# Output product of a gated convolution: sums of weights on VectorE, the last pair's operands kept in SBUF, first halves of x loaded, weights split up to eleven products ahead

## The chip, the cores and the metric

The kernel runs on one core of a Trainium2 chip, as one launch. The metric is the device time in microseconds. The engines have names as in the profile: PE is TensorE (PEld its weight loads), DVE is VectorE, ACT is ScalarE, POOL is GpSimd, SP is the engine whose queue issues most loads.

## The reference, cut to what matters

A decoder trunk of two layers in float32, with 1024 positions and width 1024. Layer 0 has a short gated convolution as its mixer, layer 1 a dilated attention; each is followed by a SwiGLU FFN of width 2816. The change is in layer 0's mixer alone:

```python
def short_conv_mixer(h, w_in, conv_k, w_out):
    b, c, u = jnp.split(h @ w_in, 3, axis=-1)
    y = lax.conv_general_dilated(c * u, ...)      # depthwise, causal, three taps
    return (b * y) @ w_out
# in the trunk:  x = x + short_conv_mixer(rms_norm(x, mix_norm[0]), ...)
#                x = x + swiglu(rms_norm(x, ffn_norm[0]), ...)
```

What is changed is `(b * y) @ w_out`, a product of 1024 x 1024 by 1024 x 1024, and the addition of its result to `x`.

## The kernel before, in words

**Precision.** Every float32 operand is split into a high and a low part of a narrower type (`hi`, `lo`). A product takes three matmuls: high by high, high by low, low by high (lines 656, 657, 658). `split` makes the parts of a weight: ScalarE copies the high part (line 159), VectorE subtracts it to get the low part (line 160). `hi` does the same for operands (lines 648 and 649).

**Fast products.** The large products use a Strassen-Winograd scheme: a 2 x 2 block product is done with seven products, m = 1 to 7, instead of eight. Each of the seven needs sums of blocks of the weights and sums of blocks of the operand. Rows of x and of the operand go in two halves of 512 columns ("half 0" and "half 1").

**The convolution's output product** (`down` in class `Strassen`, with key `conv`). The operand `b * y` has 8 tiles, taken as four pairs q = 0 to 3. For each pair the sums of operands for m = 4 to 7 are made by VectorE in `store` (lines 828 and 830), and all seven tiles of the pair are written to DRAM by POOL's queue (`put`, line 843, tensor `part_conv`). `feed` loads them back through SP's queue, one tile ahead (`hin`, line 865), and splits them into the operand of TensorE (`b`). The loop runs over the seven products in the order `DOWN = (1, 2, 6, 7, 4, 5, 3)`, and in each over four columns k = 0, 2, 4, 6. That makes 28 groups. One group is 12 matmuls of 128x128 by 128x512. In a group the program order is: make the weights that are due (`take`, `ensure`, four weights ahead), the matmuls, the addition of the bank to x (`add`, line 894 on ScalarE where it is the first to write that half of x, line 896 on VectorE otherwise), the rest of the convolution's own work (`drain`), one step of `feed` for the next m, and `after`.

**Weights of this product.** `add_summed` lets DMA make the sums of weight blocks. Two pages per column pair are loaded through SP's queue (line 239), and POOL's queue then adds other blocks onto them with accumulating DMAs (line 235), each after the last use of what was there before. The FFN's down product makes its sums with VectorE (`add_pair`, `combo`, line 267) from blocks loaded as they are (`raw`, line 191), each sum one weight ahead of its use.

**x.** The convolution's product consumes x before it is added to, so x comes from DRAM again: half of the first halves as plain loads through SP's queue, the rest as accumulating DMAs of POOL's queue onto the product's result (line 886).

**Into the FFN.** `after` is `entry`: after the products m = 2, 4, 5, 3 it squares the finished half tile of x (line 532), stores x to DRAM (`spill`), adds up squares, and in the last groups makes the FFN's first operands (`hcol`, line 1336, then `b`). There it also calls for FFN weights.

**Memory and order.** Each engine works through its own instructions in the order written. There are 41 pages of 128 x 1024 floats and, in this stage, 20 half pages; a new tile takes a free one and waits until its former readers are done. Queues of loads keep their order too: a load that waits for a page or for data holds up those behind it.

Of the kernel before, what the change touches and what calls it, by code (L numbers as in the profile page):

```python
# [13 lines left out]
ALU = mybir.AluOpType  # L14
# [7 lines left out]
KT = D // 128  # L22
# [28 lines left out]
FFN_PAIRS, FFN_CHUNK = 9, 3  # L51
DOWN = (1, 2, 6, 7, 4, 5, 3)
CONV_PAIRS, CONV_CHUNK = 4, 4
LEAD = 4
CONV_FEED = {(11, 7): 2, (11, 4): 1, (11, 3): 1}
CONV, QK = "conv", "qk"
QK_PAIRS = 8
# [58 lines left out]
def trunk(ctx: ExitStack, tc: tile.TileContext, x, gains_in, cwi, ck, cwo, wqkv, wo, relb,  # L116
          wg, wu, wd, oneh, ident, out):
    nc = tc.nc
# [56 lines left out]
    raw_src, raw_tile, raw_state = [], {}, [0]  # L175
    ops, made, op_state = [], {}, [0, 0]
    combos, raw_base, sums_of = {}, {}, {}
    fetch_of, fetched = {}, [0]

    def width(src):  # L180
        return math.prod(src.shape[1:])
# [15 lines left out]

    def ensure(upto):
        while op_state[0] < min(upto + 1, len(ops)):
            while fetched[0] < min(op_state[0] + 1 + LEAD, len(ops)):  # L200
                if ops[fetched[0]][0] in fetch_of:
                    fetch_of.pop(ops[fetched[0]][0])()
                fetched[0] += 1
            key = ops[op_state[0] + 1][0] if op_state[0] + 1 < len(ops) else None
            if key in sums_of:
                sums_of.pop(key)()
            made[op_state[0]] = ops[op_state[0]][1]()
            op_state[0] += 1
# [11 lines left out]
    def add_slab(key, src):  # L220
        i = len(raw_src)
        raw_src.append(src)
        ops.append((key, lambda: split(get_raw(i)[:, :width(src)])))

    def add_summed(u, ab, cd, w):


        t = {}
        block = lambda src, h: view(src, h * w, [[1, w]])
        twice = lambda src: view(src, 0, [[0, 2], [1, w]])  # L230
        pair = lambda p: view(p, 0, [[w, 2], [1, w]])
        rows = (cd.offset - ab.offset, 2)

        def accumulate(dst, src):
            nc.gpsimd.dma_start(out=dst, in_=src, accum_op=ALU.add)

        def load(name):
            t[name] = page("summed")
            nc.sync.dma_start(pair(t[name]), twice(ab) if name == "a" else view(ab, w, [rows, [1, w]]))

        def part(m):
            p = t["a" if m in (1, 7, 6, 3) else "b"]
            left, right = p[:, :w], p[:, w:2 * w]
            out = split(left if m in (1, 2, 7) else right, None, nc.vector)
            if m == 1:
                accumulate(pair(p), twice(cd))
            elif m == 2:
                accumulate(t["a"][:, w:2 * w], block(cd, 1))
            elif m == 6:
                accumulate(right, block(ab, 1))  # L250
            elif m == 4:
                accumulate(right, block(cd, 0))
            if m in (5, 3):
                del t["a" if m == 3 else "b"]
            return out

        fetch_of["m", u, 1], fetch_of["m", u, 2] = lambda: load("a"), lambda: load("b")
        return {m: (("m", u, m), lambda m=m: part(m)) for m in WINOGRAD}

    def add_pair(u, rows, w, eng, upto, low=(), sub=ALU.subtract):  # L260

# [139 lines left out]
    def add_down(i, w):  # L401

        at = 0
        for c, qs in enumerate(chunks[CONV] if i == CONV else laid):
            n, r = len(chunks[i][c]), len(raw_src)
            span = n * 128
            src = lambda t: (w[t][:, at * 128:(at + 2 * n) * 128] if n == len(qs) else
                             view(w[t], at * 128, [[len(qs) * 128, 2], [1, span]]))
            if i == CONV:
                units = [add_summed((i, c, 2 * u), src(2 * u), src(2 * u + 1), span) for u in range(4)]  # L410
            else:
                raw_src.extend(src(2 * u + v) for v in range(2) for u in range(4))
                upto = lambda m, r=r, u=0: r + {1: 4 + u, 2: 7, 5: 8 + u, 3: 11}.get(m, 7)
                units = [add_pair((i, c, 2 * u), (r + u, r + 4 + u), span, nc.vector,
                                  lambda m, r=r, u=u: upto(m, r, u), sub=ALU.add) for u in range(4)]
            ops.extend(t[m] for m in DOWN for t in units)
            at += 2 * len(qs)
        if not plain[i]:
            return
        place = paired(FFN_PAIRS, FFN_CHUNK, FT)  # L420
        first, step = place.index(plain[i][0]), place.index(plain[i][1]) - place.index(plain[i][0])
        assert [place[first + step * j] for j in range(4)] == list(plain[i])
        for n in range(KT):
            add_slab(("d", i, n), view(w[n], first * 128, [[step * 128, 4], [1, 128]]))
# [197 lines left out]
    class Strassen:  # L622
# [4 lines left out]
        def __init__(self, key, norm, nu, chunks, plain, source):  # L627
            self.key, self.norm, self.nu = key, norm, nu
            self.early = key in (CONV, QK)
            self.order = unit_order(nu, self.early)  # L630
            self.chunks, self.source = chunks, source
            self.b = {m: [None] * 4 for m in range(1, 8)}
            self.parts = {(q, m): dram.tile([128, HALF], F32, name=f"part_{key}_{q}_{m}")
                          for q in chain(*chunks) for m in range(1, 8)}
            self.plain = {f: dram.tile([128, S], F32, name=f"plain_{key}_{f}") for f in plain}
            self.st, self.quads, self.hid, self.deep = {}, {}, {}, {}
            self.banks, self.there, self.after = set(), set(), None
            self.lead = 1 if key == CONV else 2
            self.ahead, self.now = 2, 0

# [170 lines left out]
        def store(self, q, c, g):  # L811
# [10 lines left out]
            b11, b12, b21, b22 = (self.quads.pop((q, d)) for d in ((0, 0), (0, 1), (1, 0), (1, 1)))  # L822
            t = {}

            def make(m, a, b, less=False):
                t[m] = half_page("sum")
                if less:
                    nc.vector.scalar_tensor_tensor(t[m], a, -1.0, b, op0=ALU.mult, op1=ALU.subtract)
                else:
                    nc.vector.tensor_tensor(out=t[m], in0=a, in1=b, op=ALU.subtract)  # L830
                self.put(q, m, t[m])
# [8 lines left out]
            make(4, t[6], b21, True)  # L840

        def put(self, q, m, t):
            nc.gpsimd.dma_start(self.parts[q, m], t)
            self.there.add((q, m))

        def load_x(self, *ns):
            for n in ns:
# [3 lines left out]
        def feed(self, ahead=4):  # L851

            tiles = [(c, m, k) for c, qs in enumerate(self.chunks) for m in DOWN for k in range(len(qs))]
            raw, pair, n = {}, [], 0
            for i, (c, m, k) in enumerate(tiles):
                while n < min(i + 1 + ahead, len(tiles)):
                    d, mm, j = tiles[n]
                    if d or self.key == CONV:
                        raw[n] = half_page("hin")
                    else:  # L860
                        if j % 2 == 0:
                            pair = page("hin")
                        raw[n] = pair[:, half(j % 2)]
                    assert (self.chunks[d][j], mm) in self.there
                    nc.sync.dma_start(raw[n], self.parts[self.chunks[d][j], mm])
                    n += 1
                if k == 0:
                    self.b[m] = [None] * len(self.chunks[c])
                self.hi(m, k, raw.pop(i))()
                yield  # L870
            yield from self.feed_last()

# [7 lines left out]
        def down(self, c, feed):  # L880
# [6 lines left out]

            def add(n, h, b):
                fresh = c == 0 and (n, h) not in done
                if c == 0 and X[n] is None:  # L890
                    X[n] = page("x")
                done.add((n, h))
                if fresh and not (one and (n % 2, h) == (1, 0)):
                    nc.scalar.activation(X[n][:, half(h)], b, AF.Copy, scale=-1.0 if n % 2 else 1.0)
                else:
                    nc.vector.tensor_tensor(out=X[n][:, half(h)], in0=X[n][:, half(h)], in1=b,  # L896
                                            op=ALU.subtract if n % 2 else ALU.add)

            for i, m in enumerate(DOWN):
                d = c + (i + self.lead) // len(DOWN)  # L900
                steps = range(len(self.chunks[d])) if d < len(self.chunks) else (0, 2)
                for k in range(0, KT, 2):
# [2 lines left out]
                    if m == 5:  # L905
                        r[k] = bank()
                    b = bank() if m == 2 else r[k] if m in (3, 5) else p[k]
                    self.mm((c, k), m, b, m in (1, 2, 5), 4)
                    n, h = k + (m in (5, 7, 4)), int(m in (6, 5, 7, 3))
                    add(n, h, b)  # L910
                    if c == 0 and m in ((1, 6, 7) if one else (2, 4, 5, 3)):
                        source(n, h, nc.gpsimd, accum_op=ALU.add)
                    if one and m == 1:
                        X[n + 1] = page("x")
                        source(n + 1, 0, nc.sync)
                    if m == 4:
                        del p[k]
                    self.drain(c, m, k)
                    if k // 2 in steps:
                        next(feed, None)  # L920
                    if self.after:
                        self.after(c + 1 - len(self.chunks), m, k)

# [12 lines left out]
        def run(self, start, hooks={}):  # L936
# [25 lines left out]
                self.idle(n)  # L962

            prep = []
            feed = self.feed(1 if self.key == CONV else 4)
            self.products(filled, hooks)
            for c in range(len(self.chunks)):
                self.down(c, feed)
# [1198 lines left out]
```

## Time and profile before

| what | value |
|---|---|
| median of 3 runs | 2109.78 us (2109.09 to 2111.74) |
| the profiled execution's own time | 2111.59 us |
| its span in the profile | 2109.2 us |
| PE busy | 2070.2 us (98%), 10906 matmuls |
| DVE busy | 1774.8 us (84%) |
| ACT busy | 1049.3 us (50%) |
| POOL busy | 302.3 us (14%) |
| DMA moved | 317.23 MB, mean 150 GB/s |

The output product of the convolution lies between about 243 and 344 us of the span. A row of a timeline gives start, duration, engine, line, operation, output and inputs, and in brackets how long the engine stood idle before it and what ended that. A row of windows gives a stretch, its length, the busy time of each engine with its instructions, the granted clock of TensorE (1.00 is full), the share of the DMA engines and GB/s. [...]

### The profile page before, as it was taken

Reading aid. Unit: us, or ns where it says so; the run is one execution under the profiler, and the core shown is the slowest. Engines: PE = TensorE matmul, PEld = TensorE weight load, DVE = VectorE, ACT = ScalarE, POOL = GpSimd, SP = SyncE. Lnnn points to the kernel's source line nnn. Section 1 sums busy time; section 2 is a strip of 40 time slices with the busy share of each in tenths; the row PEclk is TensorE's granted clock in tenths of the full one; section 3 lists DMA queues with packets and bytes.
Section 4 is the critical chain, followed back from the end, with each engine's and each line's share of the span. In section 5 each row is a group of like instructions: output and inputs, shape, how many; then the busy total and the mean of one; then the engine's idle time right before and its main releaser. Section 6 shows DMA issues by size and latency. Waiting matters only on the chain.

```text
span 2109.2 us, 30920 instructions
## 1 busy us (share of the span) xinstructions
PE 2070.2 (98%) x10906; PEld 1780.5 (84%) x10906; DVE 1774.8 (84%) x3334; ACT 1049.3 (50%) x1946; POOL 302.3 (14%) x421
## 2 busy tenths in 40 slices
PE   9999887999999999999999999999999999999998
PEld 7888675888888888888889999998888888888887
DVE  8898758998888897888985888987998888887896
ACT  7433346534344355536544666665644434355443
POOL 1000320001010011010222333221011101012000
PEclk9999998999999999999999999999999999999999
DMA  7333893223333288634566868956223333368532
GB/s 220 95 100 101 242 289 92 85 81 112 103 107 107 99 261 238 200 92 149 169 238 186 196 167 217 238 182 182 69 85 110 102 109 106 110 210 230 160 100 80
DMA packets 141609, 317.23 MB, mean 150 GB/s; under 512 B 16348, under 2 KB 47150, under 8 KB 141456
## 3 DMA queue, kind: packets, MB, share of 16 engines
q1 hardware_dynamic: 98304, 203.51, 32.4%
q0 software_dynamic: 35520, 97.06, 16.0%
q10 hardware_dynamic: 7632, 14.70, 1.9%
q8 instruction: 86, 1.41, 0.3%
q14 instruction: 67, 0.55, 0.1%
HBM read 218.38 MB, written 87.65 MB: 145 GB/s over the span
## 4 chain that ended last, share of the span: by engine, by line
PE 91%; DMA 3%; DVE 3%; ACT 1%; issue 1%; POOL 0%; SPq 0%; DVEq 0%; ACTq 0%; POOLq 0%
PE bank L658 21%; PE bank L656 21%; PE bank L657 21%; PE bank L1761 5%; PE bank L748 3%; PE bank L751 3%; PE bank L750 3%; PE bank L458 2%; PE bank L460 2%; PE bank L459 2%; PE bank L1630 1%; PE bank L1632 1%; PE bank L1631 1%; PE bank L1687 1%; PE bank L1686 1%
## 5 line engine op out<-in xcount | busy, mean ns | idle before, releaser
L656 PE MATMUL bank<-b,w 128*128 128x512 f32 x2176 | 852.2, 392 | 20.9 <-ACT b L648 18.9
L657 PE MATMUL bank<-b,w 128*128 128x512 f32 x2176 | 851.5, 391 | 6.8 <-DVE b L649 6.5
L658 PE MATMUL bank<-b,w 128*128 128x512 f32 x2176 | 849.8, 391 | 2.0 <-DVE w L160 1.9
L656 PEld LDWEIGHTS bank<-b,w 128*128 128x128 f32 x2176 | 410.5, 189 | 108.2 <-ACT b L648 21.5
L657 PEld LDWEIGHTS bank<-b,w 128*128 128x128 f32 x2176 | 410.3, 189 | 95.0 <-DVE b L649 10.1
L658 PEld LDWEIGHTS bank<-b,w 128*128 128x128 f32 x2176 | 410.3, 189 | 89.5 <-DVE w L160 4.4
L159 ACT ACTIVATE w<-combo 128x512 fp32r<-128x512 f32 (+2 forms) x496 | 259.0, 549 | 271.7 <-DVE combo L267 230.0
L662 ACT ACTIVATE part<-bank 128x512 f32<-128x512 f32 x192 | 114.5, 596 | 399.2 <-PE bank L658 397.4
L160 DVE TENSOR_TENSOR w<-combo,w 128x512 fp32r<-128x512 f32 (+2 forms) x496 | 286.4, 590 | 30.9 <-ACT w L159 30.7
L160 DVE TENSOR_TENSOR w<-raw,w 128x512 fp32r<-128x512 f32 (+2 forms) x324 | 180.2, 577 | 37.9 <-ACT w L159 37.8
L666 DVE TENSOR_TENSOR part<-part,bank 128x256 f32<-128x256 f32 (+1 forms) x372 | 175.0, 499 | 32.0 <-PE bank L658 18.3
L159 ACT ACTIVATE w<-raw 128x512 fp32r<-128x512 f32 (+2 forms) x324 | 162.0, 532 | 15.3 <-PE bank L751 10.2
L649 DVE TENSOR_TENSOR b<-hin,b 128x512 fp32r<-128x512 f32 x168 | 114.4, 685 | 40.1 <-ACT b L648 40.0
L896 DVE TENSOR_TENSOR x<-x,bank 128x512 f32<-128x512 f32 x152 | 103.8, 683 | 32.0 <-PE bank L658 30.8
L267 DVE TENSOR_TENSOR combo<-raw 128x512 f32<-128x512 f32 (+1 forms) x176 | 116.1, 660 | 0.0
L648 ACT ACTIVATE b<-hin 128x512 fp32r<-128x512 f32 x168 | 103.3, 619 | 24.0 <-DMA hin<-part_conv 15.6
L751 PE MATMUL bank<-b,w 128*128 128x256 f32 x288 | 81.5, 283 | 0.0
L750 PE MATMUL bank<-b,w 128*128 128x256 f32 x288 | 81.5, 283 | 0.0
L748 PE MATMUL bank<-b,w 128*128 128x256 f32 x288 | 81.3, 282 | 0.0
L458 PE MATMUL bank<-w_hi,w 128*128 128x512 f32 (+1 forms) x208 | 76.4, 368 | 0.0
L459 PE MATMUL bank<-w_lo,w 128*128 128x512 f32 (+1 forms) x208 | 74.4, 357 | 0.0
L460 PE MATMUL bank<-w_hi,w 128*128 128x512 f32 (+1 forms) x208 | 74.4, 357 | 0.0
(239 smaller groups left out, 3270.9 us busy)
## 6 DMA issues: line engine op xcount, KB each, us to landing
hin<-part SPq DMA_DIRECT2D x140, 256.0 KB, 4.4
raw<-in_ffn_w_gate SPq DMA_DIRECT2D x44, 512.0 KB, 3.8
raw<-in_ffn_w_up SPq DMA_DIRECT2D x44, 512.0 KB, 3.8
part<-sum POOLq DMA_DIRECT2D x80, 256.0 KB, 2.3
raw<-in_attn_w_qkv SPq DMA_DIRECT2D x27, 512.0 KB, 5.4
raw<-in_conv_w_in SPq DMA_DIRECT2D x24, 512.0 KB, 4.3
raw<-in_ffn_w_down SPq DMA_DIRECT2D x32, 384.0 KB, 4.8
part<-part POOLq DMA_DIRECT2D x40, 256.0 KB, 2.5
```

Source lines behind the costliest of these rows:

```text
L159: nc.scalar.activation(hi, src, AF.Copy)
L160: low = lambda: eng.tensor_tensor(out=lo, in0=src, in1=hi, op=ALU.subtract)
L458: nc.tensor.matmul(b, whi[:, a], ahi[:, s], start=first, stop=False)
L459: nc.tensor.matmul(b, whi[:, a], alo[:, s], start=False, stop=False)
L460: nc.tensor.matmul(b, wlo[:, a], ahi[:, s], start=False, stop=last)
L656: nc.tensor.matmul(b, hi[:, a], bhi, start=start and k == 0, stop=False, skip_group_check=True)
L657: nc.tensor.matmul(b, hi[:, a], blo, start=False, stop=False, skip_group_check=True)
L658: nc.tensor.matmul(b, lo[:, a], bhi, start=False, stop=k == n - 1, skip_group_check=True)
L666: nc.vector.tensor_tensor(out=t, in0=t, in1=b, op=ALU.add)
L748: nc.tensor.matmul(b, hi[:, a], bhi, start=i in (1, 2, 5) and k == 0, stop=False, skip_group_check=True)
L750: nc.tensor.matmul(b, hi[:, a], blo, start=False, stop=False, skip_group_check=True)
L751: nc.tensor.matmul(b, lo[:, a], bhi, start=False, stop=k == n - 1, skip_group_check=True)
```

## The change

- `add_summed` and its loads go. The weights of the output product are loaded as they are (eight blocks of 512 KB), and VectorE makes the sums with `add_pair`, as it does for the FFN's down product.
- The last pair (`near`) isn't written to DRAM and read back: its operand tiles stay in SBUF, the four sums of m = 4 to 7 in two pages of their own, and `feed` takes them from there. `feed` loads four tiles ahead instead of one.
- All eight first halves of x are loaded through SP's queue at the start of `down`, and VectorE adds the products m = 1, 2 and 4 to them. The second halves stay as they were (ScalarE writes, POOL's queue accumulates).
- In this product weights are made 4, 5, 7, 9, 11, 11, 11 ahead, by product in the order of `DOWN`, at most up to operation 31 counted from the product's first, that is four weights into the FFN.
- In the groups of m = 6 `feed` makes two steps instead of one.

```diff
-LEAD = 4
+AHEAD, AHEAD_TO = (4, 5, 7, 9, 11, 11, 11), 31
...
-            while fetched[0] < min(op_state[0] + 1 + LEAD, len(ops)):
-                if ops[fetched[0]][0] in fetch_of:
-                    fetch_of.pop(ops[fetched[0]][0])()
-                fetched[0] += 1
...
-    def add_summed(u, ab, cd, w):
...
-            if i == CONV:
-                units = [add_summed((i, c, 2 * u), src(2 * u), src(2 * u + 1), span) for u in range(4)]
-            else:
-                raw_src.extend(src(2 * u + v) for v in range(2) for u in range(4))
-                upto = lambda m, r=r, u=0: r + {1: 4 + u, 2: 7, 5: 8 + u, 3: 11}.get(m, 7)
-                units = [add_pair((i, c, 2 * u), (r + u, r + 4 + u), span, nc.vector,
-                                  lambda m, r=r, u=u: upto(m, r, u), sub=ALU.add) for u in range(4)]
+            raw_src.extend(src(2 * u + v) for v in range(2) for u in range(4))
+            upto = lambda m, r, u: r + {1: 4 + u, 2: 7, 5: 8 + u, 3: 11}.get(m, 7)
+            units = [add_pair((i, c, 2 * u), (r + u, r + 4 + u), span, nc.vector,
+                              lambda m, r=r, u=u: upto(m, r, u), sub=ALU.add) for u in range(4)]
...
+            two = [page("sums") for _ in range(2)] if q == self.near else []
...
-                t[m] = half_page("sum")
+                t[m] = two[m in (6, 4)][:, half(m in (5, 4))] if two else half_page("sum")
...
         def put(self, q, m, t):
-            nc.gpsimd.dma_start(self.parts[q, m], t)
-            self.there.add((q, m))
+            if q != self.near:
+                nc.gpsimd.dma_start(self.parts[q, m], t)
+            self.there[q, m] = t if q == self.near else None
...
+                    if q == self.near:
+                        continue
...
-                self.hi(m, k, raw.pop(i))()
+                q = self.chunks[c][k]
+                self.hi(m, k, self.there.pop((q, m)) if q == self.near else raw.pop(i + 1))()
...
-                if fresh and not (one and (n % 2, h) == (1, 0)):
+                if fresh and not (one and h == 0):
...
+            for n in range(KT if one else 0):
+                X[n] = page("x")
+                source(n, 0, nc.sync)
...
-                    self.mm((c, k), m, b, m in (1, 2, 5), 4)
+                    self.mm((c, k), m, b, m in (1, 2, 5), min(AHEAD[i], AHEAD_TO - 4 * i - k // 2) if one else 4)
...
-                    if c == 0 and m in ((1, 6, 7) if one else (2, 4, 5, 3)):
+                    if c == 0 and m in ((6, 7) if one else (2, 4, 5, 3)):
                         source(n, h, nc.gpsimd, accum_op=ALU.add)
-                    if one and m == 1:
-                        X[n + 1] = page("x")
-                        source(n + 1, 0, nc.sync)
...
-                        next(feed, None)
+                        for _ in range(1 + (one and i == 2)):
+                            next(feed, None)
...
-            feed = self.feed(1 if self.key == CONV else 4)
+            feed = self.feed()
```

More of the change, by code (lines that the diff above doesn't have):

```diff
@@ L177, in trunk @@
     combos, raw_base, sums_of = {}, {}, {}
-    fetch_of, fetched = {}, [0]
     def width(src):
@@ L223, in add_slab @@
         ops.append((key, lambda: split(get_raw(i)[:, :width(src)])))
-    def add_summed(u, ab, cd, w):
[L228 to L258, printed above, removed]
     def add_pair(u, rows, w, eng, upto, low=(), sub=ALU.subtract):
@@ L636, in __init__ @@
             self.st, self.quads, self.hid, self.deep = {}, {}, {}, {}
-            self.banks, self.there, self.after = set(), set(), None
+            self.banks, self.there, self.after = set(), {}, None
+            self.near = chunks[-1][-1] if key == CONV else None
             self.lead = 1 if key == CONV else 2
@@ L857, in feed @@
                     d, mm, j = tiles[n]
+                    q = self.chunks[d][j]
+                    n += 1
+                    if q == self.near:
+                        continue
                     if d or self.key == CONV:
@@ L863, in feed @@
                         raw[n] = pair[:, half(j % 2)]
-                    assert (self.chunks[d][j], mm) in self.there
-                    nc.sync.dma_start(raw[n], self.parts[self.chunks[d][j], mm])
-                    n += 1
+                    assert (q, mm) in self.there
+                    nc.sync.dma_start(raw[n], self.parts[q, mm])
                 if k == 0:
                     self.b[m] = [None] * len(self.chunks[c])
-                self.hi(m, k, raw.pop(i))()
+                q = self.chunks[c][k]
+                self.hi(m, k, self.there.pop((q, m)) if q == self.near else raw.pop(i + 1))()
                 yield
@@ L889, in add @@
                 fresh = c == 0 and (n, h) not in done
-                if c == 0 and X[n] is None:
+                if X[n] is None:
                     X[n] = page("x")
                 done.add((n, h))
-                if fresh and not (one and (n % 2, h) == (1, 0)):
+                if fresh and not (one and h == 0):
                     nc.scalar.activation(X[n][:, half(h)], b, AF.Copy, scale=-1.0 if n % 2 else 1.0)
```

## The prediction

> **What bounds the kernel now.** I read the page first, then busy time by stretches, then TensorE's waits, then the order of time around each wait. All times are of the profiled execution.
>
> ```profile
> span 2109.2 us, 30920 instructions
> ```
>
> Windows; the columns are stretch, length, busy time (with instructions) of PE, PEld, DVE, ACT, POOL, granted PE clock, DMA share, GB/s:
>
> ```profile
> 60.00:200.00 140.00, 140.00 (x619) 115.88 (x618) 121.79 (x232) 53.45 (x92) 8.15 (x15) 1.00 0.30 93
> 240.00:250.00 10.00, 9.72 (x43) 7.71 (x43) 9.93 (x21) 5.00 (x10) 5.91 (x6) 1.00 1.08 266
> 250.00:365.00 115.00, 89.82 (x356) 69.89 (x355) 71.48 (x113) 58.27 (x103) 28.68 (x35) 0.88 0.79 202
> 253.90:282.40 28.50, 16.76 (x63) 12.81 (x62) 11.36 (x18) 8.56 (x16) 10.20 (x14) 0.76 1.05 278
> 309.00:326.00 17.00, 12.80 (x43) 9.19 (x42) 11.16 (x18) 6.80 (x12) 0.00 (x0) 0.80 0.64 180
> 344.40:364.00 19.60, 12.12 (x44) 8.99 (x44) 18.09 (x29) 12.98 (x23) 3.02 (x4) 0.83 0.42 94
> ```
>
> Undisturbed, a matmul takes 140.00 / 619 = 0.226 us, so a group of 12 takes 2.71 us. The output product of the convolution is 28 such groups (7 products m, 4 columns each; I call them g0 to g27). The row from 250 to 365 holds 356 matmuls, worth 80.5 us, in 115.0 us: **34.5 us are lost here**, in waits and at a lower clock. That is the most that the change can win.
>
> TensorE in order of time, at the waits (idle before, and what ended it, in brackets):
>
> ```profile
> 255.77 0.40 PE L658 MATMUL bank<-b,w 128*128 128x512 f32 x1
> 267.91 0.79 PE L656 MATMUL bank<-b,w 128*128 128x512 f32 x1 [11.74 <-ACT b L648]
> ...
> 315.07 0.50 PE L657 MATMUL bank<-b,w 128*128 128x512 f32 x1 [0.90 <-DVE b L649]
> 315.41 0.40 PE L658 MATMUL bank<-b,w 128*128 128x512 f32 x1
> 318.43 0.80 PE L656 MATMUL bank<-b,w 128*128 128x512 f32 x1 [2.62 <-ACT b L648]
> ...
> 334.10 0.50 PE L656 MATMUL bank<-b,w 128*128 128x512 f32 x1 [0.86 <-ACT b L648]
> 335.50 0.50 PE L657 MATMUL bank<-b,w 128*128 128x512 f32 x1 [0.90 <-DVE b L649]
> ...
> 348.15 0.79 PE L656 MATMUL bank<-b,w 128*128 128x512 f32 x1 [3.70 <-ACT b L648]
> 351.88 0.80 PE L657 MATMUL bank<-b,w 128*128 128x512 f32 x1 [2.94 <-DVE b L649]
> ```
>
> Three places. What stands behind the first two is in the waits of SP's queue and of ScalarE (total us, times, longest), and in the order of time:
>
> ```profile
> SPq L865 <- DMA part_conv<-y: 29.6, 2, 22.4
> ACT b L648 <- DMA hin<-part_conv: 15.6, 2, 12.7
> ACT w L159 <- DMA summed<-in_conv_w_out: 6.4, 2, 4.3
> ```
>
> ```profile
> 251.43 1.24 POOL L843 DMA_DIRECT2D part_conv<-y  x1
> 261.43 0.33 SPq L865 DMA_DIRECT2D hin<-part_conv  x1
> 267.22 0.63 ACT L648 ACTIVATE b<-hin 128x512 fp32r<-128x512 f32 x1 [12.66 <-DMA hin<-part_conv]
> ```
>
> First, the last pair's operand goes through DRAM: stored at 251.43, read back from 261.43, used at 267.22, with the DMA engines full (share 1.05). Second, at 312 to 318 ScalarE waits for weights that POOL's accumulating DMAs finish late, and the operands queued behind them are late too. Third, from 334 on, VectorE and ScalarE are behind TensorE.
>
> **The change, part by part.**
>
> *Last pair kept on chip.* Seven POOL stores and seven SP loads go. The first stall's cause goes whole: g4 no longer waits for 267.22. What is late next is VectorE, which stands full while the last pair's gating is finished (9.93 of 10 us in the row from 240) and has these rows at the end; g3 ends at the bank release of the ACT row:
>
> ```profile
> 253.96 0.60 ACT L894 ACTIVATE x<-bank 128x512 f32<-128x512 f32 x1 [1.08 <-PE bank L658]
> 254.70 0.69 DVE L649 TENSOR_TENSOR b<-hin,b 128x512 fp32r<-128x512 f32 x1
> 255.30 0.68 DVE L160 TENSOR_TENSOR w<-summed,w 128x512 fp32r<-128x512 f32 x1
> ```
>
> ```profile
> 203.25 0.68 DVE L267 TENSOR_TENSOR combo<-raw 128x512 f32<-128x512 f32 x1
> 203.97 0.69 DVE L267 TENSOR_TENSOR combo<-combo,raw 128x512 f32<-128x512 f32 x1
> 204.58 0.69 DVE L160 TENSOR_TENSOR w<-combo,w 128x512 fp32r<-128x512 f32 x1
> ```
>
> From start to start, such a VectorE instruction takes 0.60 us (254.70 to 255.30), and a pair of combos 1.33 us (203.25 to 204.58).
>
> *First halves of x loaded.* ScalarE loses four copies in g0 to g3, VectorE gains four adds (4 x 0.60 = 2.40 us), POOL loses four accumulating DMAs, SP gets eight loads in a row instead of four spread ones.
>
> *Sums by VectorE.* POOL loses 16 accumulating DMAs (12 of 256 KB, four of 512 KB) and with them the second stall; SP's eight loads stay eight of 512 KB. VectorE gains 16 adds: two per column for m = 6, one for m = 7, one for m = 3. They are queued one weight ahead.
>
> So VectorE's order, from its end of 255.9 before the change: 2.40 for the four adds, 1.33 for the first pair of combos, 0.60 for the last operand's low part of m = 2: done at 260.2. TensorE ends g3 at 253.9 and can run g4 until it needs the third low part (257.1 instead of 255.6: **1.5 us**) and the fourth (260.2 instead of 258.0: **2.2 us**). In g4 VectorE then has two pairs of combos, two weights' low parts, the add to x and an operand: 2.66 + 4 x 0.60 = 5.1; in g5 1.33 + 1.80 = 3.1; in g6 and g7 one combo each, 0.7 + 1.80 = 2.5. That puts the last operand of m = 6 at 273.4, while TensorE, from g4's end at 260.8, wants it at 271.2: **2.2 us**, with 0.4 for the third counted in. g8 ends at 273.8 instead of 253.9 + 5 x 2.71 = 267.5: 6.3 us lost. From g8 to g19 VectorE has the low parts of 18 weights and 16 operands, 6 combos, four adds to x and four of squares, 48 x 0.60 = 29 us against 12 x 2.71 = 32.5, so it catches up.
>
> *Weights up to eleven ahead, second operand per group in m = 6.* No instruction more, only an earlier place (operands' loads too are issued four ahead instead of one): 3 weights are made in g8, g12 and g16, two in g4. Operands for m = 5 and m = 3 are done four groups earlier, which is what the wait at 315 to 318 lacked. In the last eight groups no convolution weight is split any more. That bears on the third place. VectorE there:
>
> ```profile
> 344.19 0.68 DVE L896 TENSOR_TENSOR x<-x,bank 128x512 f32<-128x512 f32 x1
> ...
> 346.08 0.69 DVE L160 TENSOR_TENSOR w<-raw,w 128x512 fp32r<-128x512 f32 x1 [0.61 <-ACT w L159]
> 346.69 0.74 DVE L1336 SCALAR_TENSOR_TENSOR hcol<-x,gains,rstd 128x512 f32<-128x512 f32 x1
> 347.35 0.68 DVE L649 TENSOR_TENSOR b<-hcol,b 128x512 fp32r<-128x512 f32 x1
> 347.96 0.68 DVE L896 TENSOR_TENSOR x<-x,bank 128x512 f32<-128x512 f32 x1
> ...
> 351.14 0.68 DVE L649 TENSOR_TENSOR b<-hcol,b 128x512 fp32r<-128x512 f32 x1
> 351.75 0.68 DVE L896 TENSOR_TENSOR x<-x,bank 128x512 f32<-128x512 f32 x1
> ```
>
> One turn is 347.96 - 344.19 = 3.77 us, over 2.71, so VectorE falls behind. Without the weight and the wait before it, a turn is 2.5 us; the last two keep a weight of the FFN and stay at 3.2 to 3.8. VectorE reaches the add of g27 about 0.6 us after TensorE's end, instead of 7 (351.75, against TensorE's end at 348.15 - 3.70 = 344.4). The first low part for the FFN stands just ahead of this add: wanted 0.2 us after g27's end, there at 0.6, **0.4 us**. The third stands five instructions later, at 3.7, and is wanted at 2.0: **1.7 us**. Together 2.1, where the window from 344.4 shows 19.6 - 44 x 0.226 = 9.6 us lost now.
>
> *What the loads cost.* SP's order becomes raws, operands, eight halves of x, the last raw; the FFN's first two raws, issued at 201.70 now, move behind all of it.
>
> ```profile
> 201.70 3.05 SPq L191 DMA_DIRECT2D raw<-in_ffn_w_gate  x2
> ...
> 235.68 0.42 SPq L886 DMA_DIRECT2D x<-in_x  x1
> ```
>
> ```profile
> raw<-in_ffn_w_gate SPq DMA_DIRECT2D x44, 512.0 KB, 3.8
> x<-in_x SPq DMA_DIRECT2D x20, 256.0 KB, 5.8
> ```
>
> ```profile
> DMA to landing us min/median/max: 2.0/8.4/16.6
> ```
>
> The last row is that of all x loads from 230 to 345, POOL's among them. x's first half is wanted after g0, at 253.9 - 3 x 2.71 = 245.8. Issued by 238 (now 235.68, after a wait of SP that goes) and landing after 5.8, SP's own median, it is in time with 2 us of cover; I cost it at nothing. Beyond that each us late is a us on VectorE and so on g4: at most 238 + 16.6 - 245.8 = 8.8 us. A gain here is excluded, since nothing waits for x now. The FFN's raws are wanted at g17, near 298; pages fall free from g13, near 287, and 3.8 later they are there: nothing, with 7 us of cover.
>
> Sum: 6.3 + 2.1 = 8.4 us lost instead of 34.5: **26 us less**. The profiled execution took 2111.59 us (2.4 around its span), 1.8 above the median of 2109.78; taken from the median, that is 2084. After 365 TensorE runs without gaps, so the gain is kept.
>
> **The clock.** In 309 to 326 the granted clock fell to 0.80 by waits of 0.90 and 2.62 us with two matmuls between. My waits of 1.5 and 2.2 us with three between are a little shorter. If they do the same, some 7 us at half clock cost 3.4, of which 2.2 lie under VectorE's lateness at g8: 1.2 to 3.4 us more. [...]
>
> **Rivals.**
> - *Half clock at g4*: 2085 to 2088. For it, the row of 309 to 326; against it, the two waits of 0.86 and 0.90 us at 334 did not lower it (the matmuls from 335.50 take 0.50 and less, not 0.80).
> - *VectorE has room*: its instructions slip into others' waits, g4 and g8 wait under 2 us together: 34.5 - 4 = 30 us, 2079; with nothing lost, 2075. Against it: 9.93 of 10.
> - *x or the raws late*: six raws, eight halves of x and five operands are 6.5 MB, at 266 GB/s some 24 us from 222 on, so DMA is about full. The 8.8 us above give 2093.
> - *No gain*: a load takes the place of the one removed, and g4 waits as long as now, since x lands near 258 only and VectorE's 14 us stand behind it. The first place's 28.5 - 63 x 0.226 = 14.3 us stay; of the other 20 half is still gained, 2100; with the tail's turns unchanged too, it is 2108.
> - *Slower*: the FFN's first raws stand in SP's queue behind all hin loads and wait for pages, of which twelve now hold weights. ScalarE blocks in g17 on the raw, and with it the operands of m = 3. The cover is the raw's 7 us and m = 5's 10.8; it turns slower from a landing past 298 + 11 + 26 = 335. Landing at 345 gives 2120. Against it: from the code I count at most 38 of 41 pages in use in g17 to g20.
>
> **How the numbers follow.** Chances: forecast 0.56 (2080 to 2088), half clock 0.13, room 0.12, loads late 0.10, no gain 0.05 (0.03 of it within 0.2%), slower 0.04. The range leaves out the best 0.06 and the last 0.10: 2077 to 2095. 0.2% (4 us) is about what a measurement of this kernel can tell from no change: faster 0.92, same 0.04, slower 0.04.
>
> **What would show it.** Right: no wait over 3 us between 250 and 330; two waits of TensorE on VectorE's operands in g4, one in g8; VectorE full from 240 to 273; the FFN starting near 326. Wrong: ScalarE or VectorE waiting for DMA of x or raw, a clock under 1 past 270, SP waiting for pages with raws behind it.

## The result and the profile after

| what | before | after |
|---|---|---|
| median | 2110.22 us (2109.09 to 2111.74, 4 runs) | 2098.30 us (2092.25 to 2099.07, 4 runs) |
| ratio | | 0.9937 (95%: 0.9917 to 0.9956) |
| the profiled execution, its span | 2111.59, 2109.2 us | 2099.07, 2097.3 us |
| DVE busy | 1774.8 us | 1786.8 us |
| DMA moved | 317.23 MB | 308.31 MB |

The kernel became 12 us faster. Forecast were 26, with a range from 15 to 33: the direction is right, the size less than half. Six further runs of the same kernel, beside another set of runs of the kernel before, gave 2094.19 us (first experiment below). Over all ten runs it lies between 2090.8 and 2099.1 us, five of them from 2098.0 to 2099.1.

The windows of the kernel after, to hold against those of before; the columns are as above (stretch, length, PE, PEld, DVE, ACT, POOL, granted clock, DMA share, GB/s):

```profile
250.00:365.00 115.00, 105.51 (x434) 84.80 (x433) 100.74 (x163) 68.99 (x121) 13.80 (x16) 0.94 0.48 131
253.90:282.40 28.50, 24.60 (x96) 19.42 (x96) 27.45 (x45) 15.36 (x28) 4.34 (x5) 0.88 0.46 115
309.00:326.00 17.00, 14.70 (x57) 11.43 (x56) 11.09 (x18) 9.01 (x15) 1.84 (x3) 0.90 0.46 123
328.00:344.40 16.40, 13.11 (x50) 10.01 (x49) 15.52 (x26) 10.47 (x18) 1.73 (x3) 0.90 0.46 104
980.00:990.00 10.00, 7.19 (x19) 5.07 (x19) 9.87 (x17) 8.93 (x17) 0.00 (x0) 0.66 0.00 0
```

A matmul at a granted clock of 1.00 costs 0.226 us (140.00 us with 619 of them from 60 to 200, in the kernel after as before; each record lasts 0.39 us, so one overlaps the next). So length minus count x 0.226 is what a stretch loses:

| stretch | lost | forecast |
|---|---|---|
| 253.9 to 282.4, groups g4 to g9 | 28.5 - 96 x 0.226 = 6.8 us | 6.3 |
| 309 to 326, statistics of the FFN's norm | 17 - 57 x 0.226 = 4.1 us | 0 |
| 328 to 344.4, end of the stage | 16.4 - 50 x 0.226 = 5.1 us | 2.1 |
| 980 to 990, layer 1, far behind the stage | 10 - 19 x 0.226 = 5.7 us | 0 |

The excess over the forecast is 0.5 + 4.1 + 3.0 + 5.7 = 13.3 us; 26 less 13.3 is 12.7, and the two profiled executions differ by 12.5. So these four places account for nearly all of the miss. Not counted are 1.0 us that the kernel before loses too around the work of the fourth place (994 to 1004, 10 - 40 x 0.226), and a wait of 0.82 us at 957.82 in the kernel after, which adds about as much.

TensorE at the waits, in order of time, from the kernel after:

```profile
257.21 0.50 PE L615 MATMUL bank<-b,w 128*128 128x512 f32 x1 [1.73 <-DVE b L607]
260.34 0.79 PE L615 MATMUL bank<-b,w 128*128 128x512 f32 x1 [2.17 <-DVE b L607]
...
311.89 0.50 PE L528 MATMUL bank<-sum,ones_r 128*128 128x512 f32 x1 [2.05 <-ACT sum L516]
312.64 0.50 PE L528 MATMUL bank<-sum,ones_r 128*128 128x512 f32 x1 [0.25 <-DVE sum L520]
...
332.50 0.50 PE L615 MATMUL bank<-b,w 128*128 128x512 f32 x1 [1.18 <-DVE b L607]
336.28 0.50 PE L615 MATMUL bank<-b,w 128*128 128x512 f32 x1 [2.11 <-DVE b L607]
...
982.24 0.71 PE L528 MATMUL bank<-sum,ones_r 128*128 128x512 f32 x1 [2.12 <-ACT sum L516]
983.65 1.65 PE L528 MATMUL bank<-sum,ones_r 128*128 128x512 f32 x3 [0.69 <-DVE sum L520]
```

The 11.74 us for the last pair's operand are gone. At all four places two waits follow each other closely, and with one of the two, or within 1.1 us behind the second, matmuls begin to take 0.6 to 0.8 us instead of 0.4. The granted clock is 0.50 there: from 258.73 to 265.55, 313.35 to 316.76, 337.24 to 340.65 and 982.36 to 989.18.

**The first place** went as forecast. VectorE's rows in order of time, for the last operand of m = 2 and of m = 6:

```profile
259.60 0.68 DVE L607 TENSOR_TENSOR b<-y,b 128x512 fp32r<-128x512 f32 x1
...
272.87 0.69 DVE L607 TENSOR_TENSOR b<-sums,b 128x512 fp32r<-128x512 f32 x1
```

They are done at 260.28 and 273.56; forecast were 260.2 and 273.4. `b<-y` and `b<-sums` show that these operands no longer come through `hin`.

**The second place** is new. VectorE from 295 on, and what hangs on it at the end:

```profile
295.32 0.69 DVE L227 TENSOR_TENSOR combo<-raw,combo 128x512 f32<-128x512 f32 x1
295.92 0.69 DVE L160 TENSOR_TENSOR w<-combo,w 128x512 fp32r<-128x512 f32 x1
296.52 0.69 DVE L227 TENSOR_TENSOR combo<-raw,combo 128x512 f32<-128x512 f32 x1
297.12 1.48 DVE L160 TENSOR_TENSOR w<-combo,w 128x512 fp32r<-128x512 f32 x2
298.51 0.68 DVE L861 TENSOR_TENSOR x<-x,bank 128x512 f32<-128x512 f32 x1
...
309.97 0.68 DVE L861 TENSOR_TENSOR x<-x,bank 128x512 f32<-128x512 f32 x1
...
311.90 0.69 DVE L520 TENSOR_TENSOR sum<-acc,sum 128x512 fp32r<-128x512 f32 x1
```

Three weights' low parts and two sums, 3.2 us, stand ahead of the addition to x at 298.51. This is g16, the first group of m = 4, where the number of weights ahead goes from 9 to 11. The groups of m = 4 finish a half of x; ScalarE squares each tile of it after VectorE's addition, and the total is the input of the matmul at line 528, which TensorE has in its order between two groups.

**The fourth place** lies in layer 1, where the change touches no line. POOL's queue, ScalarE and VectorE of the kernel after, and ScalarE of the kernel before at the same piece of work (a small table, copied in pieces of up to 512 columns):

```profile
942.93 0.85 POOL L1177 DMA_DIRECT2D acc<-sq  x1 [4.55 <-DMA acc<-sq]
...
946.48 1.29 ACT L561 ACTIVATE low<-bank 16x512 f32<-16x512 f32 x3
953.11 0.35 ACT L561 ACTIVATE low<-bank 16x217 f32<-16x217 f32 x1 [5.33 <-DMA acc<-sq]
...
953.49 0.37 DVE L562 TENSOR_TENSOR t<-bank,low 16x217 f32<-16x217 f32 x1 [4.25 <-ACT low L561]
```

```profile
964.28 1.53 ACT L604 ACTIVATE low<-bank 16x512 f32<-16x512 f32 x4
```

Before, the four copies follow each other. After, the fourth `low` gets a half page whose former content, a tile of squares, is still being read by an accumulating DMA of POOL's queue (the row at 942.93). ScalarE stands for 5.33 us, VectorE for 4.25, and the square sums behind them are late for the matmuls at 982 and 983.

### The profile page after: what moved, and what is told of

It reads as the page before. It is cut to its first block, busy times and chain, and to the rows that moved or that the text cites. A ratio compares the mean times of both kernels' runs of the same rounds, so it can differ in the third digit from the quotient of the medians.

```text
span 2097.3 us, 30865 instructions
## 1 busy us (share of the span) xinstructions
PE 2070.6 (99%) x10906; PEld 1782.8 (85%) x10906; DVE 1786.8 (85%) x3354; ACT 1047.2 (50%) x1942; POOL 279.5 (13%) x394
## 2 busy tenths in 40 slices
DMA packets 136201, 308.31 MB, mean 147 GB/s; under 512 B 15868, under 2 KB 46670, under 8 KB 136048
## 4 chain that ended last, share of the span: by engine, by line
PE 52%; DVE 2%; ACT 0%; issue 0%; DVEq 0%; ACTq 0%
PE bank L616 10%; PE bank L615 10%; PE bank L614 10%; PE bank L1727 5%; PE bank L415 2%; PE bank L416 2%; PE bank L417 2%; PE bank L1596 2%; PE bank L1598 1%; PE bank L1597 1%; PE bank L709 1%; PE bank L708 1%; PE bank L706 1%; PE bank L1653 1%; PE bank L1652 1%
## 5 line engine op out<-in xcount | busy, mean ns | idle before, releaser
L159 ACT ACTIVATE w<-combo 128x512 fp32r<-128x512 f32 (+2 forms) x512 | 268.9, 551 | 281.5 <-DVE combo L227 241.1
L160 DVE TENSOR_TENSOR w<-combo,w 128x512 fp32r<-128x512 f32 (+2 forms) x512 | 298.5, 596 | 31.7 <-ACT w L159 31.2
L160 DVE TENSOR_TENSOR w<-raw,w 128x512 fp32r<-128x512 f32 (+2 forms) x336 | 189.0, 583 | 36.0 <-ACT w L159 35.6
L159 ACT ACTIVATE w<-raw 128x512 fp32r<-128x512 f32 (+2 forms) x336 | 169.3, 535 | 15.5 <-PE bank L709 10.5
L607 DVE TENSOR_TENSOR b<-hin,b 128x512 fp32r<-128x512 f32 x161 | 109.8, 687 | 18.6 <-ACT b L606 18.4
L227 DVE TENSOR_TENSOR combo<-raw 128x512 f32<-128x512 f32 (+1 forms) x184 | 122.1, 663 | 0.0
L606 ACT ACTIVATE b<-hin 128x512 fp32r<-128x512 f32 x161 | 98.7, 619 | 9.4 <-DMA hin<-part 5.8
```

The costliest lines, as they stand in the source:

```text
L159: nc.scalar.activation(hi, src, AF.Copy)
L160: low = lambda: eng.tensor_tensor(out=lo, in0=src, in1=hi, op=ALU.subtract)
L227: eng.tensor_tensor(out=c, in0=a, in1=b, op=op)
L607: return lambda: eng.tensor_tensor(out=lo, in0=t, in1=hi, op=ALU.subtract)
```

## The experiments

Medians are beside the median of the kernel before on the same chip and in the same set of runs. "Against after" is the end of the last matmul in the one profiled execution against that of the kernel after's first profile; for a place on the way it is the start of the same matmul in both.

| kernel | median (us) | before | difference | ratio (95%) |
|---|---|---|---|---|
| after, again | 2094.19 | 2112.19 | -18.0 | 0.9919 (0.9906 to 0.9931) |
| table summed in place | 2093.06 | 2112.19 | -19.1 | 0.9911 (0.9897 to 0.9925) |
| eleven ahead from m = 7 | 2088.88 | 2112.19 | -23.3 | 0.9892 (0.9879 to 0.9905) |
| weights up to operation 33 | 2095.09 | 2112.19 | -17.1 | 0.9919 (0.9906 to 0.9932) |
| last pair through DRAM | 2105.43 | 2113.60 | -8.2 | 0.9957 (0.9939 to 0.9976) |
| four weights ahead throughout | 2103.39 | 2113.60 | -10.2 | 0.9954 (0.9938 to 0.9971) |
| x half by POOL as before | 2096.01 | 2113.60 | -17.6 | 0.9915 (0.9900 to 0.9930) |
| first three together | 2086.02 | 2113.60 | -27.6 | 0.9871 (0.9856 to 0.9886) |
| before, last pair kept alone | 2101.32 | 2112.02 | -10.7 | 0.9949 (0.9933 to 0.9966) |
| the three and x half by POOL | 2086.56 | 2112.02 | -25.5 | 0.9878 (0.9863 to 0.9893) |
| the last, fewer ahead in m = 2 | 2082.59 | 2112.02 | -29.4 | 0.9862 (0.9847 to 0.9876) |
| one step of `feed` in m = 6 | 2095.34 | 2112.02 | -16.7 | 0.9918 (0.9901 to 0.9935) |

**The kernel after again.** No edit.

> The changed kernel once more, unaltered, for the spread of its own runs: three were at 2098 to 2099 us and one at 2092.25. Theory 'table': in layer 1's start ScalarE waits 5.3 us for a half page that an accumulating DMA still reads, and with it some matmuls run at half clock; that depends on how late this DMA lands, so most runs lie near 2098 and a few near 2092. [...]

Two of its six runs lie at 2098.70 and 2099.06, four between 2090.79 and 2094.85; the profiled one, 2099.06, has the same four waits as the first profile. With the first set that makes five runs within 1.1 us at the top, then 3.2 us without a run, then five spread over 4.1: not the "most" near 2098 and the "few" near 2092 of theory 'table'. The granted clock is 0.998 in the run of 2090.79 and 0.993 in that of 2099.06, so half clock comes and goes as well; but 0.995 stands beside 2093.53 and 2098.70 alike. So a single median of this kernel is good to some 4 us only, and the experiments below are read by the profile first.

**The table summed in place.** No `low` needs a half page any more:

```diff
-            b, low = bank(), half_page("low")
+            b, low = bank(), t[g][:H, c0 - g * G0:c1 - g * G0]
...
-            nc.scalar.activation(low[:H, :w], b[64:64 + H, :w], AF.Copy)
-            nc.vector.tensor_tensor(out=t[g][:H, c0 - g * G0:c1 - g * G0], in0=b[:H, :w], in1=low[:H, :w], op=ALU.add)
+            nc.scalar.activation(low, b[64:64 + H, :w], AF.Copy)
+            nc.vector.tensor_tensor(out=low, in0=b[:H, :w], in1=low, op=ALU.add)
```

> The changed kernel, with the position tables of layer 1 summed in place instead of through four half pages named low. Theory 'table': the wait of 5.3 us on the accumulating DMA is gone, with it the wait for the sums of squares at 982 and the half clock behind it: 5 to 6 us less, 2092 to 2093 in all runs. Rival 'clock': that wait is hidden and the half clock there is chance; under 1 us less, and runs on both sides of 2095.

ScalarE's copies in its order of time, and TensorE's waits between 930 and 1000 (engine, line, what it waited for, total, times, longest):

```profile
945.61 1.53 ACT L561 ACTIVATE t<-bank 16x512 f32<-16x512 f32 x4
```

```profile
PE bank L528 <- DVE sum L520: 0.2, 1, 0.2
PE bank L614 <- ACT w L159: 0.2, 1, 0.2
```

The wait and what followed from it are gone: against after the profile ends 7.1 us earlier, 6.2 of them won between 956 and 990. The median is only 1.1 us below the runs beside it, and 5 below the first set. The four runs lie within 1.3 us instead of 8.3. Of the six other variants that leave line 559 as it is, two (eleven ahead from m = 7, and four ahead) do not show TensorE's wait of 2.1 us here in their profiles, four do. So it seems to hang on how the DMAs fall in time, and to be one source of the spread of the kernel after; that it is the only one isn't shown.

**Eleven ahead from m = 7.** The burst of weights comes four groups earlier:

```diff
-AHEAD, AHEAD_TO = (4, 5, 7, 9, 11, 11, 11), 31
+AHEAD, AHEAD_TO = (4, 5, 7, 11, 11, 11, 11), 31
```

> The changed kernel with weights 11 ahead from the product m = 7 on (4, 5, 7, 11, 11, 11, 11) instead of 9 there. Theory 'burst': in the first group of m = 4 three weights and two sums stand ahead of the addition to x, 3.2 us of VectorE, and it stays 2.5 us late through m = 4, so TensorE waits 2.9 us for the sums of squares at 312 and runs at half clock after it. Made in m = 7, where VectorE has idle time, they cost nothing: that wait shrinks to under 0.5 us, no half clock there, 3 to 5 us less (2093 to 2095). Rival 'chain': the wait comes from the order square, add, copy between ScalarE and VectorE at that place; it stays above 2 us and the time changes by under 1 us.

VectorE at g16 in order of time, and the windows that hold the statistics and the tail:

```profile
296.01 0.69 DVE L861 TENSOR_TENSOR x<-x,bank 128x512 f32<-128x512 f32 x1 [0.28 <-PE bank L616]
...
309.71 0.69 DVE L520 TENSOR_TENSOR sum<-acc,sum 128x512 fp32r<-128x512 f32 x1
```

```profile
300.00:320.00 20.00, 19.62 (x86) 15.71 (x85) 15.47 (x26) 10.92 (x20) 1.73 (x2) 1.00 0.52 163
328.00:344.00 16.00, 13.18 (x57) 10.56 (x58) 14.73 (x25) 11.49 (x20) 1.72 (x2) 1.00 0.24 49
```

At 296.01 VectorE waits for TensorE, where after it came 2.5 us later; the sum is ready 2.2 us earlier, TensorE waits 0.2 us, the clock stays at 1.00. The same weights cost nothing four groups earlier. With 5.3 us against the kernel after beside it, this is the largest of the single edits, but not all of it is the burst's. Against after the profile ends 11.7 us earlier: 3.5 are won at the statistics; 1.6 in the tail, where TensorE waits as after (1.18 and 2.12 us) and the clock yet stays at 1.00; 6.3 in layer 1, where this profile lacks the wait.

**Weights up to operation 33.** `AHEAD_TO` 33 instead of 31, two more of the FFN's weights are made early.

> The changed kernel with weights up to operation 33 instead of 31, so that the two FFN weights of the last two groups are made some groups earlier. Theory 'tail weights': each takes 0.6 us of VectorE plus a wait for ScalarE ahead of the last operands; the FFN's first group waits 1.2 and 2.1 us now and would wait 0.4 and under 0.8, without half clock behind: 2 to 4 us less (2094 to 2096). Rival 'tail chain': the operands' own chain (add, square, operand, low part) sets it; the waits stay within 0.5 us of 1.2 and 2.1.

```profile
332.46 0.50 PE L615 MATMUL bank<-b,w 128*128 128x512 f32 x1 [0.58 <-DVE b L607]
334.93 0.50 PE L615 MATMUL bank<-b,w 128*128 128x512 f32 x1 [0.81 <-DVE b L607]
```

The tail's waits fall from 3.3 to 1.4 us and the clock stays full (1.00 from 328 to 344, where the kernel after has 0.89); 3.5 us are won in this place, and the profile ends 2.7 us earlier. The median shows nothing; the kernel after's own spread of 8.3 us is larger than this.

**The last pair through DRAM.** `self.near = None`, and `feed` one tile ahead as before; sums by VectorE, x and the weights ahead as after.

> The changed kernel with the last pair sent through DRAM again (all four pairs alike, operands loaded one ahead as before the change), the rest kept. Theory 'round trip': the stored tile still has to land and come back; with DMA as full as before that is 16 us from 251, so TensorE waits about 10 us in the second product again and the time rises by 6 to 8 us over the changed kernel's. Rival 'traffic': the first stall came from the accumulating DMAs that filled the DMA engines; without them store and load take 3 + 4.4 us, the tile is there at 260, when VectorE's queue reaches it anyway, and the time stays within 2 us.

ScalarE at the tile that comes back, and TensorE at g4, in order of time:

```profile
257.12 0.63 ACT L606 ACTIVATE b<-hin 128x512 fp32r<-128x512 f32 x1 [8.79 <-DMA hin<-part_conv]
...
300.69 0.63 ACT L606 ACTIVATE b<-hin 128x512 fp32r<-128x512 f32 x1 [6.09 <-DMA hin<-part_conv]
```

```profile
257.35 0.50 PE L615 MATMUL bank<-b,w 128*128 128x512 f32 x1 [1.73 <-DVE b L607]
260.48 0.80 PE L615 MATMUL bank<-b,w 128*128 128x512 f32 x1 [2.16 <-DVE b L607]
```

Its wait for the statistics, from the waits of 250 to 365 (total, times, longest):

```profile
PE bank L528 <- ACT sum L516: 8.2, 1, 8.2
```

TensorE's waits at g4 are those of after, to 0.01 us. The tile still goes through DRAM, but without the 16 accumulating DMAs of the sums (and four of x, which this run doesn't part from them) it is there at 257.12 instead of 267.22, in time for VectorE's order. So the first stall needs one of the two edits, not the one to which the prediction gave it. Both together win no more there. What keeping the pair is worth beside the rest comes later: at 300.69 a tile loaded one ahead is late, TensorE waits 8.2 us for the statistics, and their matmul starts 6.6 us later than after's. The loads four ahead belong to that too; the two weren't parted.

**Before, the last pair kept alone.** The kernel before with `near`, its two pages and nothing else of the change.

> The kernel before, with one part of the change alone: the last pair's operands stay on chip; sums by accumulating DMA, x and weights as before. Theory 'either part suffices for the first stall': the tile is ready at 251 and its parts stand next in VectorE's queue, free at 256.0, so the wait of 11.7 us and the half clock behind it go (13 to 14 us in that place); but the accumulating DMAs move the same bytes in less time, so the weights that came late at 312 to 318 come later against TensorE, and half or more of it is given back there: 4 to 9 us faster than before. Rival 'accumulation sets the pace': all is given back at those weights, within 2 us of before. Rival 'near alone': nothing is given back, 12 to 14 us faster.

```profile
250.00:280.00 30.00, 26.73 (x101) 19.87 (x100) 17.42 (x29) 14.09 (x26) 12.11 (x14) 0.89 1.11 243
300.00:320.00 20.00, 19.00 (x84) 15.16 (x82) 16.93 (x27) 11.67 (x21) 0.86 (x1) 1.00 0.70 201
328.00:344.00 16.00, 8.48 (x26) 5.76 (x26) 14.74 (x24) 10.05 (x18) 1.71 (x2) 0.72 0.34 88
```

The first stall goes by this edit too, 10.7 us by the median: nearly what the whole change first showed. In its place 30 - 101 x 0.226 = 7.2 us are lost, behind a wait of ScalarE for `summed` of 4.55 us at 260.10. The second stall goes as well, though all 16 of POOL's sums are still there: from 300 to 320 TensorE loses 20 - 84 x 0.226 = 1.0 us, where before lost 17 - 43 x 0.226 = 7.3 in its window of 309 to 326. So nothing was given back at the weights that came late before. The tail keeps its loss of 16 - 26 x 0.226 = 10.1 us.

**Four weights ahead throughout.** `AHEAD, AHEAD_TO = (4, 4, 4, 4, 4, 4, 4), 99`.

> The changed kernel with all weights of this product four ahead, as before the change. Theory 'tail weights': VectorE's turn in the last groups is 3.8 us again and it enters the FFN 7 us behind, where the first group then waits some 7 us instead of 3.3; against that the burst of three weights in the first group of m = 4 is gone and with it the wait for the sums of squares (2.9 us and half clock). Together 1 to 4 us slower than the changed kernel. Rival 'no matter': the sums by VectorE four ahead are enough and the tail stays: 3 to 5 us faster than the changed kernel.

TensorE in order of time in the tail:

```profile
334.07 0.80 PE L614 MATMUL bank<-b,w 128*128 128x512 f32 x1 [5.82 <-ACT b L606]
337.80 0.79 PE L615 MATMUL bank<-b,w 128*128 128x512 f32 x1 [2.94 <-DVE b L607]
```

Until the tail it is 2.8 us ahead of the kernel after (no burst in g16), in the tail it loses 9.0 more. The early weights' worth lies there, as the prediction had it. By its end the profile is level with after, 0.2 us behind, since it lacks the wait in layer 1.

**x half by POOL as before.** Four first halves are written by ScalarE and accumulated by POOL's queue again:

```diff
-                if fresh and not (one and h == 0):
+                if fresh and not (one and (n % 2, h) == (1, 0)):
...
-                source(n, 0, nc.sync)
+                if n % 2:
+                    source(n, 0, nc.sync)
...
-                    if c == 0 and m in ((6, 7) if one else (2, 4, 5, 3)):
+                    if c == 0 and m in ((1, 6, 7) if one else (2, 4, 5, 3)):
```

> The changed kernel with the even tiles' first halves of x added by POOL's accumulating DMA to ScalarE's copy of the product m = 1 again, instead of loaded first and added to by VectorE. Theory 'VectorE bound': its four adds of 0.6 us in the first product are gone, the last operand of m = 2 is ready 2.4 us earlier, and so is the last of m = 6: the two waits in the second product shrink from 4.1 to 1.7 us and the third product starts 2.4 us earlier: 2 to 3 us faster. Rival 'x late': the accumulations land after VectorE's adds of m = 2 want them and hold up VectorE there: 0 to 3 us slower.

```profile
258.20 0.50 PE L615 MATMUL bank<-b,w 128*128 128x512 f32 x1 [1.57 <-DVE b L607]
...
271.47 0.50 PE L615 MATMUL bank<-b,w 128*128 128x512 f32 x1 [0.91 <-DVE b L607]
```

With four adds (2.4 us) less on VectorE, one wait is left at g4, the clock stays full (1.00 from 250 to 280), and 4.6 us are won at g4. At g8, where VectorE had hidden the half clock, 2.3 stay. So VectorE's order sets the first place, and the first halves of x as loads cost 2.3 us there; the median doesn't separate this from the kernel after.

**One step of `feed` in m = 6.** `for _ in range(1)`.

> The changed kernel with one operand step per group in m = 6 instead of two, so that operands are made one product ahead to the end. Theory 'slack': VectorE stands idle 3.7 us in the middle of m = 5, and the four operands of m = 3 fit there: within 1 us. Rival 'tail': they stand ahead of the FFN's operands as before the change, where TensorE waited 0.9 and 0.9 us for the last of them and VectorE fell behind: 2 to 4 us slower than the changed kernel.

Within 1.3 us of the kernel after's difference: the second step brings nothing that can be measured here.

**Together.** The first three edits; then with x half by POOL; then that with `AHEAD = (4, 4, 7, 11, 11, 11, 11)`.

> The changed kernel with three of the edits together: weights 11 ahead from m = 7 on, up to operation 33, and the position tables summed in place. By the waits that each took away: 2088.9 with 11 ahead from m = 7 on, less 2.3 for the FFN's first group; the tables add nothing where their wait is gone already: 2086 to 2087, in a spread under 3 us. If the waits hide one another, no better than 2088.9.

> The three edits together (2086.0) and besides them the even tiles' first halves of x added by POOL's accumulating DMA again. VectorE's four adds go, worth 2.3 us in the profile of that edit alone, and the half clock in the second product with them: 2083 to 2084. If the waits of VectorE on ScalarE and TensorE take their place, 2086.

> As the version before it, and weights four instead of five ahead in the second product, so that one weight and one sum fewer stand ahead of the last operand of m = 6: the third product starts up to 1.3 us earlier, 2082 to 2083. If VectorE then falls short in the third product, no change.

The three edits give 2086.02, 2 us over the forecast of the change itself. The x edit alone adds nothing: its profile has a wait of 1.9 us for the statistics again, where an operand from DRAM held up ScalarE for 3.42 us at 296.29 and with it VectorE for 2.31 at 296.96. With one weight fewer ahead in m = 2 it does: 2082.59, a difference of 29.4 us where the kernel after has 11.9 and 18.0 in its two sets of runs. It is the best of the versions. Its window over the stage:

```profile
250.00:365.00 115.00, 110.79 (x481) 89.64 (x480) 108.68 (x177) 79.11 (x140) 15.51 (x18) 1.00 0.52 135
```

481 matmuls where after had 434 and before 356, VectorE busy for 108.68 of 115 us, the clock at 1.00 throughout. 115 - 481 x 0.226 = 6.3 us are lost here still.

## Why the prediction was wrong

- *First stall, "The first stall's cause goes whole ... What is late next is VectorE".* Right, to 0.2 us in both dates and 0.5 us in the loss. Its attribution was too narrow: taking POOL's sums (and four accumulations of x) away does as much for that stall as keeping the pair.
- *Second stall, "POOL loses 16 accumulating DMAs ... and with them the second stall".* Too narrow as well: with the last pair kept alone all 16 are still there, and the stall of 309 to 326 doesn't come. Why the weights are in time then isn't shown.
- *"From g8 to g19 VectorE has ... 29 us against 12 x 2.71 = 32.5, so it catches up."* **This step failed.** The sum is an average over twelve groups; what counted was which group got the work. Three weights and two sums in g16 put the last finished half of x 2.2 us late, 2.05 + 0.25 us of waiting and a clock of 0.50 for 3.4 us behind it: 4.1 us. VectorE had in fact caught up before: between 283 and 295 it stood idle for 0.61, 1.06, 0.82 and 0.82 us, waiting for ScalarE's operands. With the same weights in g12, 0.4 us of waiting was left, at a clock of 1.00. The FFN's first matmul starts at 330.93 instead of "near 326".
- *The tail, "0.4 us", "1.7 us", "together 2.1".* Right place, two waits as said, wrong size: 1.18 and 2.11 us, and the clock made 5.1 of it. With two more weights moved out, 1.4 us of waits remained and the clock stayed at 1.00. Part of the 5.1 is luck: with eleven ahead from m = 7 waits of 1.18 and 2.12 us left the clock at 1.00.
- *"After 365 TensorE runs without gaps, so the gain is kept."* **This failed too**, by 5.7 us in the profiled run (1.0 of which before loses as well). No engine's sum could have shown it: 600 us later a tile gets a buffer that a DMA still reads, one that held it for 10.2 us from its issue. The row of before (four copies in 1.53 us) shows the place without a wait, but not how near it was.
- *The clock, "1.2 to 3.4 us more" at g4 as a rival with 0.13.* The half clock did come at g4 (0.50 from 258.73 to 265.55), and most of it lay under VectorE's lateness at g8, as that part said; with x half by POOL, one wait fewer, it didn't come. That the forecast's 2084 counts it at nothing is the author's estimate, which no run shows. And it was priced at one place alone. At the other three it added 1.8 to 2.9 us to the waits: 309 to 326 at 0.90, the tail at 0.90, layer 1 at 0.66.
- *Costed at nothing: loads of x, raws.* Right: the first halves' loads and the FFN's raws held up no compute engine: among the waits between 250 and 365 none of TensorE, VectorE or ScalarE is for a DMA.
- *Rivals "x or the raws late", "no gain", "slower".* None came in the form given; that the measured 2098.3 is close to the 2100 of "no gain" is chance, since its cause (x late for g4) didn't occur.

What stays open: which part of the change brings layer 1's half page into conflict, the shift of the order in which half pages are taken or the shift in time. And what else there is in that kernel's spread from 2090.8 to 2099.1 us.

## What to carry to other kernels

Where an engine is said to catch up, write its work down group by group beside the dates that others need, above all where an add feeds a statistic; an average with 3 us to spare hid a loss of 4. Work moved earlier should be moved to a place where nothing on that engine is due, and where it went counted for more here than how much was moved. When a change moves the order in which buffers are taken, or the time, look at the slowest reader of each rotating buffer for the whole rest of the kernel, not for the stage alone.

## What the hardware showed

The granted clock fell to 0.50 after quite short waits. In the kernel after, behind waits of 2.05 and 0.25 us whose matmuls start 0.75 us apart, it is 0.50 from 313.35 to 316.76; the matmuls stood 0.43 us apart there instead of 0.226, for about 3.4 us:

```profile
313.51 0.63 PE L616 MATMUL bank<-b,w 128*128 128x512 f32 x1
...
316.50 0.52 PE L614 MATMUL bank<-b,w 128*128 128x512 f32 x1
316.85 0.40 PE L615 MATMUL bank<-b,w 128*128 128x512 f32 x1
```

A single wait of 1.57 us (x half by POOL, g4), and two of 0.58 and 0.81 us that lay 2.5 us apart (weights up to operation 33), did not: the clock there is 1.00. Nor does the sum of the waits tell: in the tail, 1.18 and 2.11 us brought 0.50 from 337.24 to 340.65 in the kernel after, while 1.18 and 2.12 us with eleven ahead from m = 7 left 1.00 from 328 to 344. What parts the two isn't shown.

An estimate from the four places of the kernel after: two waits of 2.3 to 3.9 us in all were followed, or overlapped, by 3.4 or 6.8 us at 0.50. Such a pair is to be priced with 1.7 us more, half of 3.4, or with 3.4, half of 6.8; whether it comes isn't known beforehand.

An accumulating DMA of 256 KB took from its issue at 942.93 until 953.11, 10.2 us, to let go of its source, while the DMA engines were nearly full; the median of such transfers, in the list of issues (KB, us to landing), is 4.1:

```profile
acc<-sq POOLq DMA_DIRECT2D x15, 256.0 KB, 4.1
```

```profile
943.00:953.00 10.00, 10.00 (x47) 8.26 (x46) 4.95 (x9) 3.35 (x7) 0.78 (x1) 1.00 0.90 288
```
